# Mixing narrow and wide weight blocks one by one in a two-layer decoder trunk

## Chip, cores and metric

The kernel runs on one core of one Trainium2 chip. The metric is device time in microseconds of one execution; lower is better. Three timed runs of the kernel before gave 772.72, 772.83 and 772.97 us.

## What is computed

A hidden state of 256 tokens by 1024 channels goes through two layers, all in float32. Layer 0 mixes tokens with a gated short convolution, layer 1 with dilated attention. Behind each mixer come a squared-ReLU MLP (1024 to 4096 to 1024) and a gated per-layer embedding.

```python
def short_conv_mixer(h, w_in, w_conv, w_out):
    gate_b, gate_c, xin = jnp.split(h @ w_in, 3, axis=-1)
    y = gate_b * causal_depthwise_conv(gate_c * xin, w_conv)
    return y @ w_out

for i in range(DEPTH):            # DEPTH = 2
    hn = rmsnorm(h, norm_mix[i])
    mixed = short_conv_mixer(hn, ...) if i == 0 else dilated_attention_mixer(hn, positions, ...)
    h = h + mixed
    h = h + squared_relu_mlp(rmsnorm(h, norm_mlp[i]), mlp_w_up[i], mlp_w_down[i])
    ple_gate = jax.nn.sigmoid(rmsnorm(h, norm_ple[i]) @ ple_w_gate[i])
    h = h + ple_gate * (p[i] @ ple_w_proj[i])
return rmsnorm(h, norm_final)
```

## The kernel before

**Split products.** Every float32 operand is split into a high and a low part (`hi`, `lo`), and a product is hi*hi + hi*lo + lo*hi. ScalarE (ACT) writes the high part of the weights (`whi`, L363), VectorE (DVE) the low part (`wlo`, L302). Weights arrive in slabs of up to eight tiles of 128x128. The split buffers hold six slabs, so the split of a slab can start only when TensorE (PE) is done with the slab six before it.

**Blocks.** A block is one 128x128 weight tile against 256 tokens. `block` (L374) issues it in one of these forms. A *narrow* block ("n") is three matmuls of 256 columns into one half of a PSUM bank. A *wide* block ("w") is one matmul of 256 columns (`wlo` against the high part of x) and one of 512 (`whi` against high and low part side by side) into a bank of its own; afterwards `sums` (L414) adds the two halves of that bank, with an ACT copy and a DVE addition for each of the two column blocks. In "w" every second block (`half`) has its two matmuls in reverse order, so that two of 512 columns stand behind each other, and then two of 256. A third form ("t") has the tokens as stationary operand and is not touched.

**The plan.** `make_plan` writes out one list for the whole program: blocks, and steps ("do", ...) such as `conv`, `mix_out`, `gate_out`, `squares`, `stat`. A scheduler then sets each engine's order from that list; each engine runs its own order strictly. Steps named in `URGENT` (L33) go ahead of others. The stages are: the input product of the convolution (`conv_in`, matrices C, B and X, four column pairs c), its output product (`mix`, four column pairs j), the MLP of layer 0 (`mlp_plan`), the gate (`gate_plan`), attention with the products of q, k and v, its output product (`w_o`), the MLP of layer 1, and the last gate.

**The norms.** `h_ready` (L437) makes the operand x of the next product from h[j]: two ACT and two DVE instructions, and then, but for the first norm, `squares` (an ACT square, one or two DVE additions). When the four squares are summed, `stat` (L477) or `stat_rows` (L494) takes the sum over channels with a small matmul. `gate_out(j)` (L632) multiplies the gate's product by a row of norm factors, takes the sigmoid, multiplies, adds to h, and calls `h_ready(3, j)`; attention's first product reads that x3_j. `mix_out(1, j)` (L609) makes x4_j for the MLP of layer 1 in the same way.

Of the kernel before, what the change touches and what calls it, by code (L numbers as in the profile page):

```python
# [49 lines left out]

def head_start(key, name, operand, out, stat=None):

    plan = []
    for kp in range(NP):
        if stat and kp == NP - 2:
            plan.append(("do", "stat", stat))
        for j in (0, 1):
            for k in (2 * kp, 2 * kp + 1):
                for i in (0, 1):
                    plan.append(("w", key, k, 2 * j + i, (name, j), i, operand))  # L60
            if stat and kp == NP - 1 and j == 0:
                plan.append(("do", "spread", stat))
    return plan + [("do", *out, 0), ("do", *out, 1)]


def mlp_plan(layer):
    up, down, x = f"up{layer}", f"down{layer}", f"x{3 * layer + 1}"
    plan = head_start(up, "u", x, ("up_out",))
    for j in range(2, FF // P // 2):
# [4 lines left out]
        if j == 3:  # L74
            plan.append(("do", "stat_rows", 3 * layer + 1))
        if (layer, j) == (0, 8):
# [62 lines left out]
def make_plan():  # L139
# [3 lines left out]
    def conv_in(what, c, ks):  # L143
        s = "BCX".index(what)
        return [
            ("w" if c > 1 and (what, c) != ("B", 3) or what == "X" else "n", "sc_in", k, s * NK + 2 * c + i, (what, c), i, "x0")
# [4 lines left out]
    for kp in range(NP):  # L151
        for what in "CBX":
            plan += conv_in(what, 0, (2 * kp, 2 * kp + 1))
            if what == "C" and kp + 1 < NP:
                plan.append(("do", "x_in", kp + 1))
            if what == "B":
                plan.append(("do", "squares", 0, kp))
    plan.append(("do", "add_up", ("X", 0)))
    for c in range(1, NP):
        plan += conv_in("C", c, range(2))  # L160
        plan += [("do", "stat", 0)] if c == 1 else []
        plan += conv_in("C", c, range(2, NK)) + ([("do", "add_up", ("C", c))] if c > 1 else []) + conv_in("X", c, range(3))
        plan += [("do", "spread", 0), ("do", "conv", 0)] if c == 1 else []
# [3 lines left out]
    def mix(key, j, ks):  # L167
        return [("n", key, k, 2 * j + i, ("o", j), i, "y") for k in ks for i in (0, 1)]

    for k in range(6):  # L170
        plan += mix("sc_out", 0, (k,)) + mix("sc_out", 1, (k,))
    for j in range(NP):
        plan += mix("sc_out", j, range(6 if j < 2 else 0, NK)) + [("do", "mix_out", 0, j)]
# [37 lines left out]
    def w_o(kj):  # L211

        return [
            ("w" if j < 2 else "n", "w_o", k, 2 * j + i, ("o", j), i, "y") for k, j in kj for i in (0, 1)
        ]


    plan += w_o((k, j) for k in range(3) for j in range(3)) + [("do", "scores", last)]
    plan += w_o([(k, j) for k in (3, 4) for j in range(3)] + [(k, 3) for k in range(5)]) + [("do", "turn", last)]
    plan += w_o((5, j) for j in range(NP)) + [("do", "last_values")]  # L220
# [40 lines left out]
def tile_trunk(ctx: ExitStack, tc: tile.TileContext, plan, slabs, ap, out):  # L261
# [54 lines left out]
    for op in plan:  # L316
        if op[0] != "do":
            key = ((*op[4], op[5]), 0) if op[0] == "w" else (op[4], op[5] if op[0] == "n" else 0)
# [55 lines left out]
    def block(kind, key, k, col, name, half, operand, m=0, cuts=1):  # L374
        name = (*name, half) if kind == "w" else name
# [10 lines left out]
        elif kind == "w":  # L386
# [4 lines left out]
            products = products[::-1] if half and (key != "qkv" or col[1] or not col[2]) else products  # L391
# [45 lines left out]
    def h_ready(n, j):  # L437
# [7 lines left out]
        if n:  # L445
# [142 lines left out]
    def conv(c):  # L588
# [5 lines left out]
        pb = sums(("B", c), b) if c == 2 else close(("B", c))  # L594
# [353 lines left out]
```

## Time and profile before

| | |
|---|---|
| median of 3 runs | 772.83 us (772.72 to 772.97) |
| the profiled execution | 772.91 us; its span from first to last instruction 771.1 us |
| PE (matmul), busy | 762.9 us, 99%, 4828 instructions |
| PE weight load, busy | 686.6 us, 89% |
| DVE, busy | 595.4 us, 77% |
| ACT, busy | 483.8 us, 63% |
| DMA | 140.84 MB, 183 GB/s |

The ends of matmuls are modelled and neighbours overlap in the pipeline. So this document reads PE by the distance from one matmul's start to the next, not by busy time.

### The profile page before, as it was taken

The numbers are of one execution on the slowest core, as the hardware profiler recorded it, in microseconds if no ns is written. First come the engines' busy times: TensorE is split into PE (matmuls) and PEld (weight loads), VectorE is DVE, ScalarE is ACT, GpSimd is POOL, SyncE is SP. The second block draws the span as 40 slices with busy tenths as digits, with TensorE's granted clock in tenths as the row PEclk, the third lists the DMA queues.
The fourth block names the chain that finished last, engine by engine and source line by source line (L and its number), as shares of the span: only waits on it lengthen the run. The fifth ranks groups of instructions, "written<-read, shape, count | busy, mean of one in ns | idle before, by whom it ended". The sixth has DMA issues, their size and how long they took to land. (4 is left out here: it accounts for less than half of the span.)

```text
span 771.1 us, 12612 instructions
## 1 busy us (share of the span) xinstructions
PE 762.9 (99%) x4828; PEld 686.6 (89%) x4828; DVE 595.4 (77%) x953; ACT 483.8 (63%) x782; POOL 8.9 (1%) x22
## 2 busy tenths in 40 slices
PE   9999999999999999999999999999999999999996
PEld 9998998888888899989989989989988888888885
DVE  6898779898566668898988978977798887555664
ACT  7655565565444446688887778777575555444454
POOL 0000000000000000000000000000000000000002
PEclk9999999999999999999999999999999999999999
DMA  8855555555555554554556456446456555555521
GB/s 304 311 199 188 188 180 186 189 189 194 190 191 191 189 186 145 185 189 149 174 169 195 151 166 191 154 157 220 137 178 203 193 191 187 184 188 191 185 91 56
DMA packets 42541, 140.84 MB, mean 183 GB/s; under 512 B 4849, under 2 KB 6385, under 8 KB 42481
## 3 DMA queue, kind: packets, MB, share of 16 engines
q1 hardware_dynamic: 41904, 139.39, 53.5%
q8 instruction: 38, 0.62, 0.3%
q10 hardware_dynamic: 576, 0.66, 0.3%
q14 instruction: 23, 0.18, 0.1%
HBM read 138.97 MB, written 1.05 MB: 182 GB/s over the span
## 5 line engine op out<-in xcount | busy, mean ns | idle before, releaser
L302 DVE TENSOR_TENSOR wlo<-raw,whi 128x1024 fp32r<-128x1024 f32 (+2 forms) x277 | 319.4, 1156 | 135.4 <-ACT whi L363 132.6
L363 ACT ACTIVATE whi<-raw 128x1024 fp32r<-128x1024 f32 (+2 forms) x277 | 278.0, 1007 | 183.4 <-PE acc_d L399 77.1
L399 PE MATMUL acc_u<-x,whi 128*128 128x512 f32 x512 | 160.8, 396 | 0.0
L399 PE MATMUL acc_d<-u,whi 128*128 128x512 f32 x512 | 160.8, 395 | 0.0
L399 PE MATMUL acc_qk<-x,whi 128*128 128x512 f32 x384 | 124.6, 395 | 0.0
L399 PEld LDWEIGHTS acc_d<-u,wlo 128*128 128x128 f32 x512 | 96.2, 188 | 22.7
L399 PEld LDWEIGHTS acc_u<-x,wlo 128*128 128x128 f32 x512 | 96.0, 188 | 22.8 <-ACT x L442 0.4
L399 PE MATMUL acc_u<-x,wlo 128*128 128x256 f32 x512 | 101.6, 278 | 0.1
L399 PE MATMUL acc_d<-u,wlo 128*128 128x256 f32 x512 | 100.9, 278 | 0.0
L399 PE MATMUL acc_qk<-x,wlo 128*128 128x256 f32 x384 | 86.9, 280 | 0.0
L399 PEld LDWEIGHTS acc_qk<-x,wlo 128*128 128x128 f32 x384 | 72.1, 188 | 12.1
L399 PEld LDWEIGHTS acc_u<-x,whi 128*128 128x128 f32 x512 | 78.0, 189 | 0.2
L399 PEld LDWEIGHTS acc_d<-u,whi 128*128 128x128 f32 x512 | 77.9, 189 | 0.0
L399 PE MATMUL acc_v<-whi,x 128*128 128x384 f32 x256 | 67.2, 337 | 0.0
L399 PEld LDWEIGHTS acc_qk<-x,whi 128*128 128x128 f32 x384 | 62.5, 188 | 4.6
L399 PEld LDWEIGHTS acc_v<-whi,x 128*128 128x128 f32 x256 | 46.5, 188 | 0.1
L399 PE MATMUL acc_o<-y,whi 128*128 128x256 f32 (+1 forms) x224 | 44.7, 299 | 0.0
L399 PE MATMUL acc_v<-wlo,x 128*128 128x384 f32 x128 | 42.9, 335 | 0.0
L418 ACT ACTIVATE r<-acc_u 128x256 f32<-128x256 f32 x64 | 23.8, 373 | 24.6 <-PE acc_u L399 24.4
L650 ACT ACTIVATE rot<-qk 16x512 f32<-16x512 f32 x48 | 30.3, 632 | 9.9 <-DVE qk L419 9.2
L399 PEld LDWEIGHTS acc_o<-y,whi 128*128 128x128 f32 x224 | 34.8, 191 | 0.0
L399 PE MATMUL acc_o<-y,wlo 128*128 128x256 f32 x128 | 33.7, 284 | 0.0
(175 smaller groups left out, 976.7 us busy)
## 6 DMA issues: line engine op xcount, KB each, us to landing
raw<-in_w SPq DMA_DIRECT2D x230, 512.0 KB, 3.3
raw<-in_w SPq DMA_DIRECT2D x32, 384.0 KB, 3.6
raw<-in_w SPq DMA_DIRECT2D x10, 256.0 KB, 5.3
h<-in_xT SPq DMA_DIRECT2D x4, 256.0 KB, 5.5
gain<-in_gain SPq DMA_DIRECT2D x2, 256.0 KB, 4.6
out<-htg SPq DMA_DIRECT2D x2, 256.0 KB, 2.1
mask<-in_mask SPq DMA_DIRECT2D x2, 192.0 KB, 4.1
raw<-in_w ACTq DMA_DIRECT2D x2, 128.0 KB, 4.2
```

What stands on the lines that cost most here:

```text
L302: nc.vector.tensor_tensor(out, a, f32(b), ALU.subtract)
L363: nc.scalar.activation(hi[:, :width], t[:, :width], AF.Copy)
L399: nc.tensor.matmul(to, a, b, start=n == 0 and name not in opened, stop=n == len(products) - 1 and left[name, half if kind == "n" else 0] == 0,
L418: nc.scalar.activation(t[:, i, :], p[:, 1, :], AF.Copy)
L650: nc.scalar.activation(r[dst : dst + 16], p[src : src + 16], AF.Copy)
```

## The change

Four things change in the plan. (1) In the convolution's input product, blocks of B (narrow now for every c) and X are taken in turn by a new helper `mixed`; C stays a run of its own. (2) In the convolution's output and in the gate, half of the column pairs become wide (j = 0 and 3, and j = 0 and 2), and wide and narrow blocks are taken in turn; in attention's output the existing wide and narrow blocks are taken in turn. (3) The wide blocks of these stages have a new kind "m": as "w", but always with 256 columns first. (4) `h_ready` no longer calls `squares` for norms 1 and 4 (those of the MLPs); the plan calls it behind `up_out(2)` to `up_out(5)`, and `stat_rows` comes after j = 7 and not 3.

```diff
+def mixed(*lists):
+    at = [((n + 0.5) / len(x), m, op) for m, x in enumerate(lists) for n, op in enumerate(x)]
+    return [op for _, _, op in sorted(at, key=lambda e: e[:2])]
 def mlp_plan(layer):
...
-        if j == 3:
+        if j < 2 + NP:
+            plan.append(("do", "squares", 3 * layer + 1, j - 2))
+        if j == 3 + NP:
             plan.append(("do", "stat_rows", 3 * layer + 1))
 def gate_plan():
     def gate(j, ks):
-        return [("n", "gate0", k, 2 * j + i, ("g", j), i, "x2") for k in ks for i in (0, 1)]
+        return [("n" if j % 2 else "m", "gate0", k, 2 * j + i, ("g", j), i, "x2") for k in ks for i in (0, 1)]
-    plan = gate(0, range(6)) + gate(1, range(4)) + [("do", "stat", 2)] + gate(1, (4, 5)) + gate(0, (6, 7))
+    plan = mixed(gate(0, range(6)), gate(1, range(4))) + [("do", "stat", 2)] + mixed(gate(0, (6, 7)), gate(1, (4, 5)))
     plan += [("do", "spread", 2), ("do", "gate_out", 0)] + gate(1, (6, 7)) + [("do", "gate_out", 1)]
-    return plan + [x for j in (2, 3) for x in (*gate(j, range(NK)), ("do", "gate_out", j))]
+    plan += mixed(gate(2, range(NK)), gate(3, range(5))) + [("do", "gate_out", 2)]
+    return plan + gate(3, range(5, NK)) + [("do", "gate_out", 3)]
 def make_plan():
...
-            ("w" if c > 1 and (what, c) != ("B", 3) or what == "X" else "n", "sc_in", ...)
+            ("m" if what == "X" else "w" if what == "C" and c > 1 else "n", "sc_in", ...)
...
-        plan += conv_in("X", c, range(3, NK)) + [("do", "add_up", ("X", c))] + conv_in("B", c, range(NK))
-        plan.append(("do", "conv", c))
+        bx = mixed(conv_in("B", c, range(NK)), conv_in("X", c, range(NK)))
+        plan += bx[:6] + ([("do", "spread", 0), ("do", "conv", 0)] if c == 1 else [])
+        plan += bx[6:] + [("do", "add_up", ("X", c)), ("do", "conv", c)]
...
+        return [("n" if j in (1, 2) else "m", "sc_out", k, 2 * j + i, ("o", j), i, "y") for k in ks for i in (0, 1)]
+    plan += mixed(mix(0, range(6)), mix(1, range(6)), mix(2, range(4)))
+    plan += mixed(mix(0, (6, 7)), mix(1, (6, 7)), mix(2, (4, 5))) + [("do", "mix_out", 0, 0), ("do", "mix_out", 0, 1)]
+    plan += mixed(mix(2, (6, 7)), mix(3, range(4))) + [("do", "mix_out", 0, 2)]
+    plan += mix(3, range(4, NK)) + [("do", "mix_out", 0, 3)]
...
-            products = products[::-1] if half and (key != "qkv" or col[1] or not col[2]) else products
+            products = products[::-1] if kind == "w" and half and (key != "qkv" or col[1] or not col[2]) else products
...
-        if n:
+        if n not in (0, 1, 4):
             squares(n, j)
...
     def gate_out(j):
         s = act(f"gs{j}")
-        nc.vector.tensor_tensor(s, close(("g", j)), both(rows[2]), ALU.mult)
+        g = close(("g", j)) if ("g", j) in acc else sums(("g", j), s)
+        nc.vector.tensor_tensor(s, g, both(rows[2]), ALU.mult)
```

In the first part of the convolution's input product, PE's order was the following; `acc_B` and `acc_X` are the accumulators of matrices B and X.

```order
L399 MATMUL acc_B_253<-x_0_164,wlo_192 128x256
L399 MATMUL acc_B_253<-x_0_164,whi_191 128x256 x2
L399 MATMUL acc_X_0_274<-x_0_164,wlo_214 128x256
L399 MATMUL acc_X_0_274<-x_0_164,whi_213 128x512
L399 MATMUL acc_X_1_287<-x_0_164,whi_213 128x512
L399 MATMUL acc_X_1_287<-x_0_164,wlo_214 128x256
```

It is now:

```order
L414 MATMUL acc_B_253<-x_0_164,wlo_192 128x256
L414 MATMUL acc_B_253<-x_0_164,whi_191 128x256 x2
L414 MATMUL acc_X_0_261<-x_0_164,wlo_192 128x256
L414 MATMUL acc_X_0_261<-x_0_164,whi_191 128x512
L414 MATMUL acc_B_253<-x_0_164,wlo_192 128x256
L414 MATMUL acc_B_253<-x_0_164,whi_191 128x256 x2
L414 MATMUL acc_X_1_267<-x_0_164,wlo_192 128x256
L414 MATMUL acc_X_1_267<-x_0_164,whi_191 128x512
```

Four matmuls of 256 columns now stand between two of 512; before, X's blocks stood in pairs and B's in runs.

At the end of the gate, DVE's order from `gate_out(2)` to x3_3 was the following; `gs` are the gates, `hr` the new h, `x3_j` the low part of attention's operand, `tot` the sums of squares.

```order
L634 TENSOR_TENSOR gs2_3253<-acc_g_2_3192,row_2_3145 128x512
L455 TENSOR_TENSOR tot3_1_3189<-tot3_1_3189,tot3_0_3161 128x256
L302 TENSOR_TENSOR wlo120_3356<-raw120_3193,whi120_3355 128x1024
L636 TENSOR_TENSOR gs2_3253<-gs2_3253,prj2_223 128x512
...
L302 TENSOR_TENSOR wlo122_3405<-raw122_3271,whi122_3404 128x768
L636 TENSOR_TENSOR gs3_3331<-gs3_3331,prj3_231 128x512
L642 TENSOR_TENSOR hr3_3335<-h3_86,gs3_3331 128x256 x2
L302 TENSOR_TENSOR wlo123_3427<-raw123_3301,whi123_3426 128x768
L443 SCALAR_TENSOR_TENSOR x3_3_3338<-hr3_3335,gains_73,x3_3_3338 128x256 x2
```

It is now:

```order
L317 TENSOR_TENSOR wlo120_3325<-raw120_3173,whi120_3324 128x1024
L434 TENSOR_TENSOR gs2_3261<-acc_g_2_0_3172,gs2_3261 128x256
L434 TENSOR_TENSOR gs2_3261<-acc_g_2_1_3185,gs2_3261 128x256
L650 TENSOR_TENSOR gs2_3261<-gs2_3261,row_2_3121 128x512
L317 TENSOR_TENSOR wlo121_3351<-raw121_3200,whi121_3350 128x768
L652 TENSOR_TENSOR gs2_3261<-gs2_3261,prj2_223 128x512
...
L317 TENSOR_TENSOR wlo123_3396<-raw123_3250,whi123_3395 128x768
L652 TENSOR_TENSOR gs3_3300<-gs3_3300,prj3_231 128x512
L658 TENSOR_TENSOR hr3_3304<-h3_86,gs3_3300 128x256 x2
L317 TENSOR_TENSOR wlo124_3418<-raw124_3322,whi124_3417 128x768
L458 SCALAR_TENSOR_TENSOR x3_3_3307<-hr3_3304,gains_73,x3_3_3307 128x256 x2
```

Two additions stand ahead of gate 2's chain, and every gate stands one slab's split later in the order: split 120 comes before the first instruction of gate 2, and split 124 and not 123 is the last one ahead of x3_3. The bank of `acc_g_2_0` is the next one that attention's accumulator `acc_qk_0_2_1` takes; before, that accumulator took the bank of `acc_g_1`.

ACT's order at the beginning of that chain, behind the row of norm factors (`row_2`), was:

```order
L363 ACTIVATE whi115_3126<-raw115_2981 128x1024
L512 ACTIVATE row_2_3145<-spread_2_3142 128x256
L635 ACT_TABLE_LOAD
L635 ACTIVATE gs0_3147<-gs0_3147 128x512
L363 ACTIVATE whi116_3195<-raw116_3021 128x1024
```

It is now:

```order
L378 ACTIVATE whi115_3104<-raw115_2972 128x1024
L433 ACTIVATE gs0_3123<-acc_g_0_0_3011 128x256
L433 ACTIVATE gs0_3123<-acc_g_0_1_3024 128x256
L527 ACTIVATE row_2_3121<-spread_2_3118 128x256
L378 ACTIVATE whi116_3175<-raw116_3012 128x1024
L651 ACT_TABLE_LOAD
L651 ACTIVATE gs0_3123<-gs0_3123 128x512
```

Two copies for `sums` are added, and the split of slab 116 stands ahead of the table load and the first sigmoid, no longer behind it. In PE's order at x3_3's first use, three matmuls of 256 columns that need only its high part stand ahead of the first that needs the low part (one before), and `stat(3)` stands behind four blocks of that x and not two.

## Rows read from the trace of the kernel before

**Rows 1.** The page's busy times by engine, and the answer on what PE waited for: engine, line, what it waited for, then us in total, times, longest.

```profile
PE 762.9 (99%) x4828; PEld 686.6 (89%) x4828; DVE 595.4 (77%) x953; ACT 483.8 (63%) x782; POOL 8.9 (1%) x22
PE warm L526 <- DVE power L522: 1.0, 1, 1.0
```

**Rows 2.** Stretches of the span: the convolution's output (narrow blocks alone) and the MLP of layer 0 (wide ones alone). Columns: from and to, length, then busy us and count of PE, PE's weight load, DVE, ACT and POOL, then granted clock, DMA share and GB/s.

```profile
80.10:103.10 23.00, 23.00 (x194) 23.00 (x193) 19.23 (x29) 13.86 (x20) 0.00 (x0) 1.00 0.51 184
103.10:281.70 178.60, 178.60 (x1028) 155.86 (x1027) 128.44 (x174) 95.13 (x135) 0.00 (x0) 1.00 0.55 189
```

**Rows 3.** Timeline of PE (start, us, what), first and last row of a run of narrow blocks: one row of wlo per block, 14 blocks from the first to the last.

```profile
41.08 0.28 PE L399 MATMUL acc_B<-x,wlo 128*128 128x256 f32 x1
...
46.12 0.28 PE L399 MATMUL acc_B<-x,wlo 128*128 128x256 f32 x1
```

**Rows 4.** The same of wide blocks in paired order (two of 256, two of 512): six blocks between these two rows.

```profile
47.06 0.39 PE L399 MATMUL acc_C<-x,wlo 128*128 128x256 f32 x2
...
49.15 0.40 PE L399 MATMUL acc_C<-x,wlo 128*128 128x256 f32 x2
```

**Rows 5.** The same of wide blocks in plain order (256, 512, 256, 512, in attention): 15 blocks between these two rows.

```profile
332.00 0.28 PE L399 MATMUL acc_qk<-x,wlo 128*128 128x256 f32 x1
...
337.20 0.27 PE L399 MATMUL acc_qk<-x,wlo 128*128 128x256 f32 x1
```

**Rows 6.** Timeline of PE in attention's output, where two narrow blocks already follow four wide ones in paired order; a round of six blocks goes from one matmul pair of 512 columns at its beginning to the next.

```profile
527.95 0.62 PE L399 MATMUL acc_o<-y,whi 128*128 128x512 f32 x2
...
529.12 0.39 PE L399 MATMUL acc_o<-y,wlo 128*128 128x256 f32 x2
...
529.94 0.28 PE L399 MATMUL acc_o<-y,wlo 128*128 128x256 f32 x1
530.05 0.63 PE L399 MATMUL acc_o<-y,whi 128*128 128x512 f32 x2
...
532.17 0.63 PE L399 MATMUL acc_o<-y,whi 128*128 128x512 f32 x2
```

**Rows 7.** Timeline of ACT at the beginning of the chain of gates (brackets: idle before it, and what ended that).

```profile
291.07 1.06 ACT L363 ACTIVATE whi<-raw 128x1024 fp32r<-128x1024 f32 x1 [2.27 <-PE acc_g L399]
292.90 0.38 ACT L512 ACTIVATE row<-spread 128x256 f32<-128x256 f32 x1 [0.77 <-PE spread L508]
293.30 1.28 ACT L635 ACT_TABLE_LOAD   x1
294.60 0.63 ACT L635 ACTIVATE gs<-gs 128x512 f32<-128x512 f32 x1
295.13 1.05 ACT L363 ACTIVATE whi<-raw 128x1024 fp32r<-128x1024 f32 x1
```

**Rows 8.** Timeline of DVE along the chain of gates, from the squares of the gate's own norm to x3_3.

```profile
288.29 0.43 DVE L455 TENSOR_TENSOR tot<-tot,tot 128x256 f32<-128x256 f32 x1
...
295.26 0.69 DVE L636 TENSOR_TENSOR gs<-gs,prj 128x512 f32<-128x512 f32 x1 [1.25 <-ACT gs L635]
...
306.46 0.68 DVE L634 TENSOR_TENSOR gs<-acc_g,row 128x512 f32<-128x512 f32 x1
...
315.94 0.94 DVE L302 TENSOR_TENSOR wlo<-raw,whi 128x768 fp32r<-128x768 f32 x1
316.80 0.86 DVE L443 SCALAR_TENSOR_TENSOR x<-hr,gains,x 128x256 fp32r<-128x256 f32 x2
...
318.03 0.43 DVE L455 TENSOR_TENSOR tot<-tot,tot 128x256 f32<-128x256 f32 x1
```

**Rows 9.** Timeline of PE from the gate's small matmuls to `stat(3)`: the second of the two matmuls in the row at 308.56 is the first into acc_qk_0_2_1; the row at 318.32 begins with the first that needs the low part of x3_3.

```profile
288.94 0.51 PE L481 MATMUL ssq<-ones,tot 128*128 128x2 f32 x4
...
292.26 0.60 PE L508 MATMUL spread<-ident,n 128*128 128x128 f32 x4
...
305.66 0.28 PE L399 MATMUL acc_qk<-x,wlo 128*128 128x256 f32 x1
...
308.56 0.63 PE L399 MATMUL acc_qk<-x,whi 128*128 128x512 f32 x2
...
318.32 0.63 PE L399 MATMUL acc_qk<-x,whi 128*128 128x512 f32 x2
...
318.90 0.50 PE L481 MATMUL ssq<-ones,tot 128*128 128x2 f32 x4
```

**Rows 10.** Timeline at the beginning of the MLP of layer 1: PE, and DVE's low part of x4_1.

```profile
555.15 0.28 PE L399 MATMUL acc_u<-x,wlo 128*128 128x256 f32 x1
...
558.75 0.62 PE L399 MATMUL acc_u<-x,whi 128*128 128x512 f32 x2
559.22 0.99 PE L399 MATMUL acc_u<-x,wlo 128*128 128x256 f32 x4
560.10 0.73 PE L399 MATMUL acc_u<-x,whi 128*128 128x512 f32 x2
560.67 0.40 PE L399 MATMUL acc_u<-x,wlo 128*128 128x256 f32 x2
...
559.56 0.89 DVE L443 SCALAR_TENSOR_TENSOR x<-hr,gains,x 128x256 fp32r<-128x256 f32 x2 [0.15 <-ACT x L442]
```

**Rows 11.** DVE additions and ACT copies of `sums`, from the timelines in attention's output.

```profile
551.97 0.77 DVE L419 TENSOR_TENSOR so<-acc_o,so 128x256 f32<-128x256 f32 x2 [1.16 <-ACT so L418]
551.56 0.73 ACT L418 ACTIVATE so<-acc_o 128x256 f32<-128x256 f32 x2 [1.67 <-PE acc_o L399]
```

More of the change, by code (lines that the diff above doesn't have):

```diff
@@ L145, in conv_in @@
         return [
-            ("w" if c > 1 and (what, c) != ("B", 3) or what == "X" else "n", "sc_in", k, s * NK + 2 * c + i, (what, c), i, "x0")
+            ("m" if what == "X" else "w" if what == "C" and c > 1 else "n", "sc_in", k, s * NK + 2 * c + i, (what, c), i, "x0")
             for k in ks for i in (0, 1)
@@ L151, in make_plan @@
     for kp in range(NP):
[L152 to L157, printed above, removed]
+        ks = (2 * kp, 2 * kp + 1)
+        plan += conv_in("C", 0, ks)
+        if kp + 1 < NP:
+            plan.append(("do", "x_in", kp + 1))
+        bx = mixed(conv_in("B", 0, ks), conv_in("X", 0, ks))
+        plan += bx[:4] + [("do", "squares", 0, kp)] + bx[4:]
     plan.append(("do", "add_up", ("X", 0)))
@@ L161, in make_plan, with mix @@
         plan += [("do", "stat", 0)] if c == 1 else []
-        plan += conv_in("C", c, range(2, NK)) + ([("do", "add_up", ("C", c))] if c > 1 else []) + conv_in("X", c, range(3))
-        plan += [("do", "spread", 0), ("do", "conv", 0)] if c == 1 else []
-        plan += conv_in("X", c, range(3, NK)) + [("do", "add_up", ("X", c))] + conv_in("B", c, range(NK))
-        plan.append(("do", "conv", c))
[L167 to L173, printed above, removed]
+        plan += conv_in("C", c, range(2, NK)) + ([("do", "add_up", ("C", c))] if c > 1 else [])
+        bx = mixed(conv_in("B", c, range(NK)), conv_in("X", c, range(NK)))
+        plan += bx[:6] + ([("do", "spread", 0), ("do", "conv", 0)] if c == 1 else [])
+        plan += bx[6:] + [("do", "add_up", ("X", c)), ("do", "conv", c)]
+    def mix(j, ks):
+        return [("n" if j in (1, 2) else "m", "sc_out", k, 2 * j + i, ("o", j), i, "y") for k in ks for i in (0, 1)]
[3 more added lines that the diff above has]
+    plan += mix(3, range(4, NK)) + [("do", "mix_out", 0, 3)]
     plan += mlp_plan(0) + gate_plan()
@@ L213, in w_o, with wide @@
         return [
-            ("w" if j < 2 else "n", "w_o", k, 2 * j + i, ("o", j), i, "y") for k, j in kj for i in (0, 1)
+            ("m" if j < 2 else "n", "w_o", k, 2 * j + i, ("o", j), i, "y") for k, j in kj for i in (0, 1)
         ]
-    plan += w_o((k, j) for k in range(3) for j in range(3)) + [("do", "scores", last)]
-    plan += w_o([(k, j) for k in (3, 4) for j in range(3)] + [(k, 3) for k in range(5)]) + [("do", "turn", last)]
-    plan += w_o((5, j) for j in range(NP)) + [("do", "last_values")]
+    def wide(ks):
+        return w_o([(k, j) for k in ks for j in (0, 1)])
+    plan += mixed(wide(range(3)), w_o((k, 2) for k in range(3))) + [("do", "scores", last)]
+    plan += mixed(wide((3,)), w_o((k, 2) for k in (3, 4))) + mixed(wide((4,)), w_o((k, 3) for k in range(5)))
+    plan += [("do", "turn", last)] + mixed(wide((5,)), w_o((5, j) for j in (2, 3))) + [("do", "last_values")]
     for j in range(NP):
@@ L374, in block @@
     def block(kind, key, k, col, name, half, operand, m=0, cuts=1):
-        name = (*name, half) if kind == "w" else name
+        name = (*name, half) if kind in "wm" else name
         if name not in opened:
@@ L593, in conv @@
         pc = cur.pop(("C", c)) if c > 1 else close(("C", c))
-        pb = sums(("B", c), b) if c == 2 else close(("B", c))
+        pb = close(("B", c))
         nc.vector.tensor_tensor(t, pc, both(rows[0, 2]), ALU.mult)
```

6 lines of the change are left out of this document (3 added, 3 removed).

## Prediction

> **What bounds the kernel now.** I read the page's busy times, then PE's waits, then PE's timeline in runs of one kind of block, and last the timelines of DVE and ACT where the PE needs their results soonest. PE is busy for 99% of the span and waits for another engine only at its very first matmul [rows 1]. Since matmul ends are modelled, a short wait could hide in that 99%; the starts tell. They stand in even steps nearly everywhere, at full granted clock [rows 2], so a change moves the time in two ways: it changes the length of those steps, or it makes an operand come late at one of the few places with little slack.
>
> The steps: a narrow block takes (46.12 - 41.08) / 14 = 0.360 us [rows 3], so 0.120 per matmul of 256 columns. A wide block in paired order takes (49.15 - 47.06) / 6 = 0.348 [rows 4], one in plain order (337.20 - 332.00) / 15 = 0.347 [rows 5].
>
> The thin places: the gate's sum of squares is done at 288.29 + 0.43 = 288.72, and PE uses it at 288.94 [rows 8, 9], 0.22 later. The first half of the low part of x3_3 is ready near 317.25 (start 316.80, half of 0.86), and PE needs it at 318.32, 1.1 later. And x4_1 comes too late: behind 559.22 four matmuls of 256 take 0.88 where they should take 0.47, and the two of 512 behind them 0.57 where 0.47 is usual; PE loses 0.51 us there while DVE makes x4_1 from 559.56 [rows 10].
>
> **Term A, kinds of block.** 32 blocks of the convolution's output and 32 of the gate become wide, 16 of B become narrow: net 48 blocks at 0.360 become 48 at 0.347 or 0.348. That is -0.6 us. Columns streamed are the same; what goes is 48 matmuls, 13 ns each, which is what a matmul costs above its columns: 0.120 less 256 columns at 2.4 GHz, 0.107 [rows 3]. The Trainium skill ("TensorE: Matmul & The Clock Gate", Back-to-back issue gap) puts that extra at 2.5 ns for a warm matmul; by it A would be an estimated -0.1 us, and the trace, with 13 ns, disagrees.
>
> **Term B, taking them in turn.** In the new order, which I counted through, there are some 125 places where a single 512 is followed by three or more matmuls of 256. No stretch of before has that order. Nearest is attention's output, where two narrow blocks follow four paired wide ones [rows 6]: its rounds take 2.10 and 2.12 us, and the parts apart would be 4 x 0.348 + 2 x 0.360 = 2.11. Within a round the seven steps from 529.12 take 0.82, 0.117 each, 3 ns below 0.120, but the 512s are that much longer. So I bound B by nothing and by 3 ns for four matmuls at each place, 125 x 0.012 = -1.5 us, and take a third, -0.5, since whole rounds gain almost nothing.
>
> **Term C, the MLP of layer 1.** Without `squares` in `h_ready`, DVE and ACT have less to do ahead of x4_1. But the new order also asks for x4_1 sooner: eight blocks of u0 and u1 come first and only three matmuls of 256 and one of 512 before its low part is needed, near 555.15 + 3.4, where before twelve blocks came first. DVE's new order has, behind the last matmul of the old product at 555.15, two additions to h at 0.6, one slab's split at 1.15 and then x4_1's first half at 0.45, with 0.25 for the matmul to end and 0.6 of x4_0 left over: ready near 555.15 + 3.6. So most of the 0.51 us goes: -0.4, bounds -0.5 and +0.1.
>
> **Term D, from the gate into attention.** This is the term that decides. Times are in the clock of before, with the end of the MLP in place.
> - PE reaches `stat(2)` after 12 wide and 8 narrow blocks, 7.05 us and not 7.2, so 0.15 sooner; the slack of 0.22 covers that.
> - `spread` then comes at 292.0 (292.26 less 0.15 and four wide blocks' 0.05, and some of B), and PE is through four more blocks near 293.9. Only then is the buffer for the split of slab 116 free: ACT's splits start some 0.25 behind PE, as that of 115 at 291.07 does [rows 7]. So ACT splits from 294.15 to 295.1, and now the table load (1.3) and the sigmoid (0.63) stand behind it: the sigmoid ends near 297.0, and DVE's second multiplication of gate 0 starts near 297.1. Before, table load and sigmoid came first and it started at 295.26 [rows 7, 8]. The chain is 1.8 late.
> - From 295.26 to 316.80 DVE shows no idle time, four gates one behind the other with eight slab splits between; so lateness stays. Added are gate 2's two additions, 0.77 [rows 11]; the last split in the chain is a short one of 768 in place of one of 1024, 0.27 less. Sum: +2.3.
> - The first addition of gate 2 frees the bank of acc_qk_0_2_1. Its place follows what was at 306.46 by 1.8 and one addition of squares: it ends near 308.9 to 309.0. PE, with a gate that is 0.43 shorter by its wide blocks and 0.1 by B, wants the bank at 308.80 - 0.55 = 308.25. Wait: 0.7 us.
> - x3_3's low part is ready near 317.25 + 2.3 = 319.5. PE wants it at 318.32 - 0.55 + 0.7, and 0.24 later for the two matmuls that now stand ahead: 318.7. Wait: 0.8 us. `stat(3)`, four blocks on at 320.8, finds its sum ready: 1.2 behind x3_3's first half, as before (318.46 against 317.25) [rows 8].
>
> D is +1.5 us. Its bounds: +0.3, if my lags on ACT are each some tenths too long, and +4.3, if the chain misses one more slab's release (below).
>
> **At no cost.** Squares moved behind `up_out(2)` to (5): one ACT square and two DVE additions for each of four steps, under 1.5 us of each engine's time per step, where DVE is idle for 50 of 178.6 us [rows 2]; if that cover were gone, some 0.9 us of DVE per step would reach PE. The convolution: X's sums now begin when B and X end together, some 2 us later, but 32 blocks (11 us) and not 24 (8.6 us) lie ahead of the first that needs its y. The new `sums` of the convolution's output run beside 20 blocks (7 us).
>
> **Sum.** -0.6 - 0.5 - 0.4 + 1.5 = 0.0 against the profiled execution's 772.91 us (span 771.1 and 1.8 around it). The median of the timed runs is 0.08 below that execution, so the forecast is 772.8.
>
> **Rivals.**
> - *The wait behind the gate stays hidden.* If ACT's split of 116 finds its buffer before the row of norm factors comes, the table load is where it was and D is near 0: 771.3. For it: DVE idles 1.25 us at 295.26, room for the two additions of gate 0 [rows 8]. Against it: slab 110 ends behind the four narrow blocks after `spread`, by the plan. With B at its far end this gives 770.3.
> - *Slower: one more slab missed.* The splits of 122 and 124 stand ahead of the high parts of x3_2 and x3_3 in ACT's order, and each waits for PE to finish a slab, eight blocks or 2.8 us. If the late chain meets such a release too late, x3_3 comes 2.8 later still: 775.6. It decides once the waits pass 1.5 + 1.55 = 3.1 us. Against it: by my times the splits of 122 and 124 have their buffer 0.3 us or more before DVE's h is there.
> - *The alternation does nothing* (B = 0, C = 0): 773.7. For it: whole rounds of 2.10 and 2.12 against 2.11 [rows 6].
> - *The narrow matmuls are bound by their weight loads, and the long ones give the loads time.* For it: the load path is busy 23.00 of 23.00 us in the narrow stretch and 155.86 of 178.60 in the wide one [rows 2], and one step of 256 ahead of a 512 shows 0.11 (529.94 to 530.05) [rows 6]. At that step for four matmuls at each place the gain is 125 x 4 x 0.010 = 5 us: 767.8. Against it: the other steps there are 0.117, and in plain wide order, where each load has a long matmul near it, a block still costs 27 ns above its 768 columns [rows 5]. The Trainium skill (same page, What happens when you issue a matmul) has loads pulled ahead of matmuls in flight into a background buffer; that agrees with both readings.
>
> **How the numbers follow.** No change that a measurement of this kernel can tell is one within 0.2%, 1.55 us: 771.3 to 774.4. Chances: forecast 0.50 (own range 771.4 to 774.0, from A's, B's and C's bounds and tenths on D), hidden 0.18, one more slab 0.16, nothing from alternation 0.10, loads 0.06. Hidden lies on the bound, so half of it counts as faster, with the loads and 0.05 of the forecast: 0.20. Slower: 0.16 and some 0.04 of the edges, 0.20. The rest, 0.60, is the same. The range runs from 770.6 to 774.6: it leaves out the loads' case and most of the slab's.
>
> **What would show it.** Right: at the first acc_qk matmuls of head 0 a gap of some 0.7 us about three us into attention, and one of 0.8 where x3_3 is first used; ACT's split ahead of a table load near 295; no gap in the first 6 us of layer 1's MLP; blocks of 256 in mixed order near 0.117 to 0.120 each. Wrong: no gap into attention (then faster by 1.5), gaps over 3 us (slower), or steps of 256 near 0.11 all through the mixed stretches.

## The result, and the profile after

The changed kernel takes 773.99 us (773.67 to 774.28), the kernel before 772.86 (772.26 to 773.29), 20 runs each: a ratio of 1.0014, 95% interval 1.0008 to 1.0021. Its profiled execution has a span of 772.0 us, before 771.1. I had forecast no change, 772.8. The time lies in my range, but the change is slower beyond the interval.

The page's busy times after, and then the answer on what PE waited for (us in total, times, longest), to be held against [rows 1]:

```profile
PE 762.8 (99%) x4780; PEld 683.5 (89%) x4780; DVE 595.9 (77%) x959; ACT 486.5 (63%) x788; POOL 8.9 (1%) x22
```

```profile
PE warm L541 <- DVE power L537: 1.0, 1, 1.0
PE acc_qk L414 <- DVE gs L434: 0.6, 1, 0.6
PE acc_qk L414 <- DVE x L458: 0.4, 1, 0.4
```

There are 48 matmuls fewer, as counted, and two new waits, both on DVE and both just into attention. PE's timeline there, against [rows 9]:

```profile
308.26 0.39 PE L414 MATMUL acc_qk<-x,whi 128*128 128x512 f32 x1
309.26 0.47 PE L414 MATMUL acc_qk<-x,whi 128*128 128x512 f32 x1 [0.61 <-DVE gs L434]
309.56 0.40 PE L414 MATMUL acc_qk<-x,wlo 128*128 128x256 f32 x2
...
318.62 0.77 PE L414 MATMUL acc_qk<-x,wlo 128*128 128x256 f32 x4
319.80 0.73 PE L414 MATMUL acc_qk<-x,whi 128*128 128x512 f32 x2 [0.41 <-DVE x L458]
320.37 0.40 PE L414 MATMUL acc_qk<-x,wlo 128*128 128x256 f32 x2
...
321.18 0.50 PE L496 MATMUL ssq<-ones,tot 128*128 128x2 f32 x4
```

Read the starts, not only the brackets. One matmul of 512 stands between 308.26 and 309.26: 1.00 us where 0.23 is usual, 0.77 lost. Four of 256 stand between 318.62 and 319.80: 1.18 where 0.47 is usual, 0.71 lost. The step behind each restart is long as well: one of 512 takes 0.30 (309.26 to 309.56), and two take 0.57 where 0.47 is usual (319.80 to 320.37), 0.07 and 0.10 more. Together that is 1.65, so each wait costs more than its bracket says.

The chain behind it, first ACT's timeline and then DVE's, against [rows 7, 8]:

```profile
294.23 1.06 ACT L378 ACTIVATE whi<-raw 128x1024 fp32r<-128x1024 f32 x1 [1.11 <-PE acc_g L414]
295.31 1.28 ACT L651 ACT_TABLE_LOAD   x1
296.60 0.63 ACT L651 ACTIVATE gs<-gs 128x512 f32<-128x512 f32 x1
```

```profile
297.27 0.69 DVE L652 TENSOR_TENSOR gs<-gs,prj 128x512 f32<-128x512 f32 x1 [0.72 <-ACT gs L651]
308.69 0.75 DVE L434 TENSOR_TENSOR gs<-acc_g,gs 128x256 f32<-128x256 f32 x2
319.26 0.88 DVE L458 SCALAR_TENSOR_TENSOR x<-hr,gains,x 128x256 fp32r<-128x256 f32 x2
```

ACT's split of slab 116 now precedes the table load, the sigmoid ends near 297.2, and DVE's second multiplication of gate 0 starts at 297.27 where it started at 295.26. By these rows it is two microseconds late there and 2.46 late at x3_3 (319.26 against 316.80). The MLP of layer 0 ends 0.10 sooner in this trace than in that of before, so in the clock of before each is 0.10 later still.

Cutting both traces at the starts of the same PE matmuls shows where the time went (lengths in us). I call the fifth stretch, from the gate into attention, the seam:

| from the first matmul of | before us | after us | difference |
|---|---|---|---|
| the convolution | 68.70 | 69.20 | +0.50 |
| its output | 23.04 | 22.80 | -0.24 |
| MLP of layer 0 | 178.60 | 178.60 | 0.00 |
| the gate | 23.92 | 23.72 | -0.20 |
| the seam: qk of head 0, to `spread(3)` | 19.29 | 20.91 | +1.62 |
| attention from there | 202.89 | 202.88 | -0.01 |
| attention's output (last) | 27.31 | 27.36 | +0.05 |
| MLP of layer 1 | 179.14 | 178.62 | -0.52 |

The sum is +1.2, the medians differ by 1.13; the start-up ahead of the convolution differs by some tenths from one profiled execution to the next, whatever the kernel (11.0 to 11.7). Stretches that no edit touches agree to 0.02 between the traces, with one exception: the convolution's part ahead of `spread(0)` took 25.39 in the kernel before and 25.72 in a later run with the same convolution. So up to some 0.2 of the convolution's +0.50 may be scatter; from `spread(0)` on it went from 43.32 to 43.62, +0.30. Against my terms: D was forecast at +1.5 and is 1.62. C was forecast at -0.4 and is -0.52; the stall of [rows 10] is gone, the four matmuls of 256 take 0.47:

```profile
559.17 0.64 PE L414 MATMUL acc_u<-x,wlo 128*128 128x256 f32 x4
559.64 0.86 PE L414 MATMUL acc_u<-x,whi 128*128 128x512 f32 x3
```

A and B together were forecast at -1.1, and the four mixed stages make +0.1 (0.50 - 0.24 - 0.20 + 0.05). That is the miss, whole but for the scatter. A mixed stretch looks like this (convolution, after; a wide block of X and a narrow one of B by turns):

```profile
42.03 0.28 PE L414 MATMUL acc_B<-x,wlo 128*128 128x256 f32 x1
...
42.74 0.28 PE L414 MATMUL acc_B<-x,wlo 128*128 128x256 f32 x1
...
43.45 0.28 PE L414 MATMUL acc_B<-x,wlo 128*128 128x256 f32 x1
```

A pair of blocks takes 0.71 us; apart, by [rows 3, 4], they would take 0.360 + 0.348 = 0.708. My first reading was that a 512 alone among 256s costs 3 ns extra. The runs in plain order below speak against that.

### The profile page after: what moved, and what is told of

The parts are those of the page before. It is cut to its first block, busy times and chain, and to the rows that moved or that the text cites. A ratio compares the mean times of both kernels' runs of the same rounds, so it can differ in the third digit from the quotient of the medians.

```text
span 772.0 us, 12534 instructions
## 1 busy us (share of the span) xinstructions
PE 762.8 (99%) x4780; PEld 683.5 (89%) x4780; DVE 595.9 (77%) x959; ACT 486.5 (63%) x788; POOL 8.9 (1%) x22
## 3 DMA queue, kind: packets, MB, share of 16 engines
HBM read 138.97 MB, written 1.05 MB: 181 GB/s over the span
## 4 chain that ended last, share of the span: by engine, by line
PE 95%; DVE 3%; issue 1%; POOL 0%; ACT 0%; POOLq 0%; DVEq 0%
PE acc_u L414 23%; PE acc_d L414 23%; PE acc_qk L414 16%; PE acc_v L414 9%; PE acc_o L414 6%; PE acc_g L414 4%; PE acc_C L414 3%; PE acc_B L414 3%; PE acc_X L414 3%; PE acc_p L414 1%; DVE wlo L317 1%; PE sc L703 1%; PE o L747 1%; PE o L757 1%; PE sc L711 1%
## 5 line engine op out<-in xcount | busy, mean ns | idle before, releaser
L414 PE MATMUL acc_o<-y,wlo 128*128 128x256 f32 x128 | 36.0, 284 | 0.0
L414 PEld LDWEIGHTS acc_o<-y,whi 128*128 128x128 f32 x192 | 31.7, 189 | 2.8
```

The costliest lines, as they stand in the source:

```text
L414: nc.tensor.matmul(to, a, b, start=n == 0 and name not in opened, stop=n == len(products) - 1 and left[name, half if kind == "n" else 0] == 0,
```

## Experiments

### The gate put back

The changed kernel with `gate_plan` as a whole as in the kernel before, its first line for one:

```diff
-        return [("n" if j % 2 else "m", "gate0", k, 2 * j + i, ("g", j), i, "x2") for k in ks for i in (0, 1)]
+        return [("n", "gate0", k, 2 * j + i, ("g", j), i, "x2") for k in ks for i in (0, 1)]
...
```

> The changed kernel with the gate's blocks alone put back: all narrow, in the order of before. Theory (the loss sits at the seam from the gate into attention, because norm factors, ACT's table load and DVE's chain of gates run 1.8 us late there): the two waits that PE shows at the first acc_qk matmuls (0.61 us for DVE's gs, 0.41 us for x) go, 1.6 us are won there, the gate takes 0.2 us more, the attention after it starts at the same place as in the kernel before or a little sooner: 772.6 us. Rival (the loss is spread over the mixed stretches of the convolution and of attention's output): nothing that can be told, 774.0 us.

Measured: 772.85 us, before in the same runs 772.89 (ratio 0.9999, 0.9990 to 1.0008). PE's only wait is the first one:

```profile
PE warm L540 <- DVE power L536: 1.0, 1, 1.0
```

The seam takes 19.30 us again. So the gate's part of the change accounts for the loss, 773.99 less 772.85 or 1.14, and by the traces the seam alone for more than that; the rest of the change comes out at no difference that can be told.

### The squares alone

On the kernel before. One more line moves with the squares, here and in the changed kernel: `rope`, the rotary angles, comes one j later in the MLP of layer 0. That stage takes 178.59 to 178.60 us either way.

```diff
-        if j == 3:
+        if j in range(2, 2 + NP):
+            plan.append(("do", "squares", 3 * layer + 1, j - 2))
+        if j == 3 + NP:
             plan.append(("do", "stat_rows", 3 * layer + 1))
-        if (layer, j) == (0, 8):
+        if (layer, j) == (0, 9):
             plan.append(("do", "rope"))
...
-        if n:
+        if n not in (0, 1, 4):
             squares(n, j)
```

> The kernel before with one edit: the squares of x1 and x4 move behind the up products, as in the changed kernel. Theory (DVE gets x4_1 done sooner): the stall of 0.5 us at the first use of x4_1 in the MLP of layer 1 goes, nothing else moves: 772.35 us. Rival (the new order of attention's output took the stall away, not the squares): 772.85 us, the stall of 0.5 us still there. Against the claim that squares beside the up products cost nothing: a new wait of PE in either up product.

Measured: 772.55 (before 772.89; 0.9996, 0.9987 to 1.0005). By the times no difference can be told; by the trace the MLP of layer 1 takes 178.71 where it took 179.14, the stall is gone and no new wait is there. So 0.43 us of C come from the squares, and at most the last 0.1 from the new order of attention's output.

### In runs, plain and paired

The changed kernel's blocks in their kinds, first without the mixing, then (last two lines) with the wide ones also in paired order:

```diff
 def mixed(*lists):
-    at = [((n + 0.5) / len(x), m, op) for m, x in enumerate(lists) for n, op in enumerate(x)]
-    return [op for _, _, op in sorted(at, key=lambda e: e[:2])]
+    return [op for x in lists for op in x]
...
-            products = products[::-1] if kind == "w" and half and (key != "qkv" or col[1] or not col[2]) else products
+            products = products[::-1] if half and (key != "qkv" or col[1] or not col[2]) else products
```

> The changed kernel with its kinds of block and the squares as they are, but the lists that were mixed one by one now taken one behind the other. Theory (each 512 alone among matmuls of 256 takes 3 ns more than in a run of wide blocks, some 125 places): the stretches of the convolution, its output and the gate get shorter by 0.3 to 0.4 us together, the waits at the seam stay and eat what the gate gains: 773.7 us. My prediction's term B (mixing saves 0.5 us, at most 1.5): 774.5 us or more. Rival (order makes no difference, the stretches are as long as mixed): 774.0 us.

> The changed kernel in runs (as in the run with the lists one behind the other), and its wide blocks of the convolution, its output, the gate and attention's output in paired order (256, 512, 512, 256) in place of plain order (256, 512, 256, 512). In runs and in plain order a wide block of the output took 0.3525 us by the trace ((22.83 - 32 x 0.360) / 32 = 0.353), not the 0.347 that I took from head 1's qk blocks. Theory (A was mis-sized: plain order costs 0.3505 to 0.3525 in these stages, paired order 0.348): convolution 0.1 to 0.2 us shorter, its output 22.66 us in place of 22.80, the gate 0.1 us shorter: 773.35 us. Rival (order within a block makes no difference, these stages' operands make wide blocks cost that): 773.7 us and the output stays at 22.80 us.

Measured: 773.71 in runs (before 772.89), 773.25 in runs and paired (before 772.98). The intervals of the two ratios overlap (1.0002 to 1.0020 and 0.9994 to 1.0012), so the traces have to decide. From `spread(0)` on the convolution takes 43.62 mixed, 43.69 in runs, 43.42 paired; its output 22.80, 22.83 and 22.67; the gate 23.72, 23.74 and 23.68. So the mixing of single blocks gains 0.02 to 0.07 us in each of these stages over the same blocks in runs, and the order within the wide block is worth some 0.5 us: paired, the three stages take 0.27, 0.16 and 0.06 less. The first run met the time of its theory, 773.7, by luck: the stages did not get shorter, but the seam did, 20.42 us against 20.91, with one wait in place of two. The timeline shows the price of plain order (convolution's output in runs; 14 blocks from the first row to the last):

```profile
98.41 0.28 PE L413 MATMUL acc_o<-y,wlo 128*128 128x256 f32 x1
98.77 0.28 PE L413 MATMUL acc_o<-y,wlo 128*128 128x256 f32 x1
99.12 0.28 PE L413 MATMUL acc_o<-y,wlo 128*128 128x256 f32 x1
99.47 0.28 PE L413 MATMUL acc_o<-y,wlo 128*128 128x256 f32 x1
...
103.36 0.28 PE L413 MATMUL acc_o<-y,wlo 128*128 128x256 f32 x1
```

(103.36 - 98.41) / 14 = 0.3536 us, with steps of 0.36, 0.35, 0.35 over and over. In attention the same order gives 0.347 [rows 5]. That is the price that I carried over, and here it doesn't hold. The theory of 3 ns for each lone 512 fell with the first of these runs: there, wide blocks stand in runs, and the stages are no shorter.

### Pairs by turns

The changed kernel with the gate as before, wide blocks in paired order, and two blocks at a time:

```diff
-    at = [((n + 0.5) / len(x), m, op) for m, x in enumerate(lists) for n, op in enumerate(x)]
+    at = [((n // 2 + 0.5) / len(x), m, op) for m, x in enumerate(lists) for n, op in enumerate(x)]
...
```

> The changed kernel with the gate as before, and in the convolution, its output and attention's output two narrow blocks by turns with two wide ones in paired order (512, 512, 256 and seven more of 256), where the change took single blocks by turns (512, 256, 256, 256, 256). In the run with pairs in the output such a round of four blocks took 1.407 us, and the kinds apart would take 2 x 0.360 + 2 x 0.348 = 1.416. Theory (taking in turn does gain, but only when the wide blocks come in pairs): the output takes 16 x 1.407 = 22.51 us where the changed kernel takes 22.80, the convolution from its second row of factors on 43.3 where that takes 43.62: 772.1 us. Rival (a round gains nothing over runs in paired order): output 22.66, convolution 43.42, 772.5 us.

Measured: 772.27 (before 772.96; 0.9992, 0.9983 to 1.0000), between the theory's time and the rival's. By the trace the convolution from `spread(0)` on takes 43.25, its output 22.59. Against the paired runs that is 0.17 and 0.08 less, so taking in turn does gain something, some 0.25 us in these two stages, once the wide blocks come in pairs. The convolution came out as forecast; the output, at 22.59, missed 22.51; by its plan 8 wide blocks of j = 3 come alone at its end, and narrow and wide are not one to one ahead of them.

### The sigmoid's table loaded early

The changed kernel with a small sigmoid behind the sine, in the first run on `ones` in place of `cosr`:

```diff
         nc.scalar.activation(cosr, k, AF.Sin)
+        early = spool.tile([P, 1], F32, tag="early", name="early")
+        nc.scalar.activation(early, cosr[:, :1], AF.Sigmoid)
```

> The changed kernel with one instruction more: a sigmoid of one column behind the rotary angles' sine, in the MLP of layer 0, so that ACT's table for the sigmoid is loaded there and not behind the split of slab 116. Theory (the table load of 1.28 us stands in the chain that makes the seam late): the first sigmoid of the gate starts 1.3 us sooner, near 295.3, DVE's chain follows by 1.3 us, PE's wait for gs goes, the one for x shrinks to 0.2 us or goes: 772.7 us. Rival (DVE's two additions and its order set the wait, the table load is covered): the waits stay, 774.0 us.

> The changed kernel with one sigmoid of one column that reads the cosine of the rotary angles, so that it can't move ahead of it: the sigmoid's table is loaded in the MLP of layer 0 and not behind the split of slab 116. (In the run before, the small sigmoid had no operand that held it and moved to the start of the kernel; the table was loaded at the gate as ever.) Theory: the first sigmoid of the gate starts 1.3 us sooner, near 295.3, DVE's chain follows, the wait for gs goes, the one for x shrinks to 0.2 us or goes: 772.7 us. Rival (DVE's additions and its order set the waits, the load is covered): 774.0 us.

Measured: 774.12 for the first, which told nothing on the table: its sigmoid ran at 3.4 us, the sine's table replaced it at 172, and the gate loaded its own as ever. The second: 773.50 (before 772.98; the ratio 1.0006, 0.9997 to 1.0014, against the changed kernel's 1.0014, 1.0008 to 1.0021), between theory and rival. The chain there, in a trace whose gate starts 0.39 later than the changed kernel's, on ACT and then on DVE:

```profile
294.62 1.06 ACT L378 ACTIVATE whi<-raw 128x1024 fp32r<-128x1024 f32 x1 [1.11 <-PE acc_g L414]
295.58 0.62 ACT L653 ACTIVATE gs<-gs 128x512 f32<-128x512 f32 x1
```

```profile
295.71 1.23 DVE L317 TENSOR_TENSOR wlo<-raw,whi 128x1024 fp32r<-128x1024 f32 x1 [0.62 <-ACT whi L378]
296.85 0.69 DVE L654 TENSOR_TENSOR gs<-gs,prj 128x512 f32<-128x512 f32 x1
```

Of PE's waits one at acc_qk is left:

```profile
PE acc_qk L414 <- DVE x L458: 0.4, 1, 0.4
```

The sigmoid starts 1.4 us sooner, DVE's multiplication only 0.8 (296.85 - 0.39 against 297.27): DVE's own part of slab 116's split now stands right ahead of it. The wait for gs goes, the one for x stays; the seam shrinks from 20.91 to 20.18. So without the table load 0.8 of the lateness of 2.0 goes, not the 1.3 expected. By these rows the rest is the late split itself, through both engines; no run moved that split alone.

### Gate 2 narrow

On the changed kernel:

```diff
-        return [("n" if j % 2 else "m", "gate0", k, 2 * j + i, ("g", j), i, "x2") for k in ks for i in (0, 1)]
+        return [("n" if j else "m", "gate0", k, 2 * j + i, ("g", j), i, "x2") for k in ks for i in (0, 1)]
```

> The changed kernel with gate 2 narrow as before, gate 0 wide: DVE's two additions for gate 2, 0.75 us, fall away, 16 blocks of the gate take 0.1 to 0.15 us more. Theory (these additions are part of the chain of DVE from the gate into attention, 0.77 of 2.3 us): the wait at the first acc_qk matmuls goes, of the 1.6 us lost at the seam 0.8 remain at x3_3: 773.3 us. Rival (only ACT's table load sets the seam): 774.1 us.

Measured: 773.29 (before 772.98; 1.0005, 0.9996 to 1.0014). The time is the one forecast, the place is not: x3_3 was to keep a loss of 0.8, but both waits at acc_qk are gone, and a new one stands at the small matmuls of `stat(3)`, for the sum of squares:

```profile
PE ssq L496 <- DVE tot L470: 0.4, 1, 0.4
```

The seam takes 19.86, so 0.56 of the 1.62 remain, for 0.14 more in the gate itself (23.86). By the traces the two additions' 0.75 us of DVE are worth more at the seam than the table load, 1.05 us against 0.73; the times of the two runs are too close to tell them apart.

### Squares and pairs: what the parts are worth without the gate

On the kernel with the squares alone:

```diff
-        return [("n", key, k, 2 * j + i, ("o", j), i, "y") for k in ks for i in (0, 1)]
+        return [("w" if j in (0, 3) else "n", key, k, 2 * j + i, ("o", j), i, "y") for k in ks for i in (0, 1)]
```

> The kernel before with the squares behind the up products, and with the convolution's output in the order of before but wide in paired order for j = 0 and 3. The gate is that of before. Theory (the squares are worth 0.3 to 0.5 us, 32 paired wide blocks 32 x 0.012 = 0.38 us, and there is no seam to lose at): 772.15 us, the output's stage 22.66 us in place of 23.04. Rival (the wide blocks' sums make x1 late, or a wide block in this stage costs what a narrow one does): 772.5 us or more.

Measured: 772.18 (before 772.98; 0.9989, 0.9980 to 0.9997). The output's stage takes 22.61, against 22.66 expected. This is the lowest median of the versions, faster than the kernel before by a tenth of a per cent; the run with pairs by turns, 772.27, can't be told from it. A round of two wide and two narrow blocks there takes (84.92 - 80.70) / 3 = 1.407, where the kinds apart take 1.416:

```profile
80.70 0.63 PE L401 MATMUL acc_o<-y,whi 128*128 128x512 f32 x2
...
84.92 0.63 PE L401 MATMUL acc_o<-y,whi 128*128 128x512 f32 x2
```

### Plain order has two prices

Four runs on the last kernel, with the MLPs' wide blocks in plain order. In three of them, at some places, three blocks are issued as 256, 256, 256, 512, 512, 512: in every j of up from 2 on and of down; in up's j = 2; in up's j = 2 and 9, with the first two j of up left paired. `hold` is true for both blocks of k = 1 and the first of k = 2 in the j named.

```diff
-            products = products[::-1] if half and (key != "qkv" or col[1] or not col[2]) else products
+            products = products[::-1] if half and key[:2] not in ("up", "do") and (key != "qkv" or col[1] or not col[2]) else products
...
+            if hold and n:
+                later.append(issue)
+            else:
+                issue()
+        if len(later) == 3:
+            while later:
+                later.pop(0)()
```

> The kernel with the squares moved and the output in pairs, with both MLPs' 768 wide blocks each in plain order in place of paired order. By the traces a wide block in plain order takes 353.9 ns in the convolution, its output and the gate, in a pattern that repeats every three blocks, and 346.6 ns in attention, in one that repeats every two. Theory one (the pattern is set by what the run of plain blocks is entered from, and only narrow blocks before it give the slow one): 346.6 ns throughout, each up product 0.2 us shorter, some 2.5 us less in all: 769.5 us. Theory two (the slow pattern belongs to these stages, the fast one to attention): 353.9 ns in both MLPs, 1,500 blocks at 5.5 ns, some 8 us more: 780 us. A third outcome: the fast pattern in one MLP and not in the other.

> The kernel with both MLPs' wide blocks in plain order (512 each, not 768 as I wrote of the run before), and once in each j of up (from 2) and down three blocks taken as 256, 256, 256, 512, 512, 512. In the run before, MLP 0 went by the slow pattern throughout (353.3 ns a block), MLP 1 changed to the fast one (346.7) behind three 512s in a row near 561.5 us and kept it to its end; its times fell into two groups, near 773.8 and near 777.0. Theory (the same code has two steady patterns; a place with three 512s in a row can turn the slow into the fast, which then lasts): with such a place every 16 or 64 blocks nearly all of both MLPs goes at 346.7, 1024 x 1.7 ns under the paired order: 770.5 us, one group of times. Rival (what turned it was something else, and three 512s in a row turn it back as often): between 773 and 777, spread out.

> As the run before it, but with one such place only in each MLP, in up's j = 2. Theory: each MLP goes by one pattern from there on, fast or slow, so times fall into groups 1.7 to 3.4 us apart, and the fastest is near 770.7 us; where the turn always succeeds there, one group at 770.7. Rival (the pattern does not last without being renewed): a time between that of the run with many places and 777.

> The kernel with the squares moved and the output in pairs; in both MLPs the first two j of up stay in paired order, the rest of up and all of down go in plain order, with three 512s in a row only in up's j = 2 and j = 9, that is where the runs before had just gone into the slow pattern (from the head and from the two matmuls of the sum of squares). In the run with such a place in every j they turned slow into fast and the next one fast into slow, by turns. Theory (a place with three 512s turns a steady slow run into the fast pattern, which lasts until the next other form of matmul): in each MLP 96 blocks of up from j = 2 and some 350 from j = 9 on at 346.7, 16 at 353.3: 450 x 1.7 ns less, 0.7 us each MLP: 770.8 us. Rival (which pattern follows such a place depends on where in the slow pattern's three blocks it falls, so either may come): an MLP, or a part of it, at 353.3 from such a place on; with both wrong throughout 776.7 us.

All plain: 776.95 us, but in two groups, 773.71 and 773.91, and four times 776.94 to 777.39. (The MLPs have 512 wide blocks each; the first expectation says 768.) The profiled execution was of the shorter group. This is the third outcome named in the expectation, one price in one MLP and the other in the other. The MLP of layer 0 has 123 blocks between the first two rows below, that of layer 1 has 123 between the last two:

```profile
103.32 0.28 PE L401 MATMUL acc_u<-x,wlo 128*128 128x256 f32 x1
146.78 0.28 PE L401 MATMUL acc_u<-x,wlo 128*128 128x256 f32 x1
...
561.36 0.28 PE L401 MATMUL acc_u<-x,wlo 128*128 128x256 f32 x1
561.48 0.86 PE L401 MATMUL acc_u<-x,whi 128*128 128x512 f32 x3
562.18 0.28 PE L401 MATMUL acc_u<-x,wlo 128*128 128x256 f32 x1
...
602.98 0.28 PE L401 MATMUL acc_u<-x,wlo 128*128 128x256 f32 x1
645.62 0.28 PE L401 MATMUL acc_u<-x,wlo 128*128 128x256 f32 x1
```

43.46 / 123 = 0.3533 against 42.64 / 123 = 0.3467: the same code, operands of the same shape, two steady patterns of steps. By these prices I estimate that an execution with both MLPs in the long pattern takes 3.3 us more (some 500 blocks at 0.0067), about what parts the two groups; no execution of the longer group was profiled. The change came behind three 512s in a row at 561.48, which the scheduler had made there by itself. With such a place in every j (773.62, 773.43 to 773.98) the pattern turned from long to short at one and mostly back at the next, by turns; the 770.5 us of the theory were missed. With one place (775.91, 775.54 to 776.41, one group and not several) it turned short at up's j = 2 in layer 0 and went long again behind the two matmuls of the sum of squares:

```profile
145.67 0.39 PE L406 MATMUL acc_u<-x,whi 128*128 128x512 f32 x1
...
147.06 0.39 PE L406 MATMUL acc_u<-x,whi 128*128 128x512 f32 x1
147.29 0.40 PE L506 MATMUL ssq<-sums,ones_r 128*128 128x256 f32 x2
...
147.64 0.40 PE L406 MATMUL acc_u<-x,whi 128*128 128x512 f32 x1
...
148.70 0.40 PE L406 MATMUL acc_u<-x,whi 128*128 128x512 f32 x1
```

Four blocks ahead of the two take 1.39 (0.347 each), three behind them 1.06 (0.353). In layer 1 the pattern was long ahead of the place and stayed long behind it.

With places at the two entries only, j = 2 and 9: 773.86, in groups of 770.83 to 771.72 (five) and 773.81 to 774.84 (seven). Its profiled execution, of the long group, shows the short pattern behind j = 9 in layer 0 (105 blocks at 0.3467 between the first two rows) and the long one behind the same place in layer 1 (99 blocks at 0.3533 between the last two):

```profile
156.08 0.28 PE L406 MATMUL acc_u<-x,wlo 128*128 128x256 f32 x1
192.48 0.28 PE L406 MATMUL acc_u<-x,wlo 128*128 128x256 f32 x1
...
608.00 0.28 PE L406 MATMUL acc_u<-x,wlo 128*128 128x256 f32 x1
642.98 0.28 PE L406 MATMUL acc_u<-x,wlo 128*128 128x256 f32 x1
```

Behind j = 2 both layers went long; ahead of j = 9 the pattern was long in layer 0 and short in layer 1, so that place turned it over in both. The rival was right: either may follow. The best execution took 770.83, the theory's 770.8, but no execution of that group was profiled, and the version can't be relied on. What inside PE decides stays open. Shown is that a pattern, once entered, lasts until matmuls of another form come, that two matmuls of 256 or a row of 512s can turn it, and that the same program can go either way.

## Why the prediction was wrong, point by point

- **What bounds the kernel.** Right: by the table the time moved with lengths of steps and with late operands at thin places. PE is busy for 99% after as before.
- **Term A failed.** The step was "32 of the output and 32 of the gate at 0.360 become 0.347 or 0.348", and the change of X's and attention's output's wide blocks from paired to plain order got no term at all. The 0.347 came from attention [rows 5], a stretch in the short pattern. In the stages that changed, plain blocks in runs take 0.3536; mixed singly, a pair of blocks takes 0.71, so a wide one some 0.350. At that price X's 64 blocks cost 0.1 to 0.2 more than paired ones and B's 16 narrow ones 0.19 more, as counted, which together is about the convolution's +0.30; the output and the gate gain 0.24 and 0.20 where 32 x 0.013 = 0.42 each was forecast. With paired blocks the output's gain is there: 22.61 to 22.67 against 23.04. The kernel before has no plain run outside attention, and there every one steps at 0.347, so its trace could not show the other price; that I took one stretch for all was the error.
- **Term B failed, in size.** Single blocks by turns save 0.1 us in all over the same blocks in runs, not 0.5, and they take 0.4 to 0.5 more than runs in paired order. [Rows 6], on which I built, has paired blocks; with pairs by turns some 0.25 us are there. The change took the pairs apart, and I carried the row over as if it hadn't.
- **Term C held**: -0.52 where -0.4 was forecast, a little past its bound of -0.5; -0.43 of it with the squares alone.
- **Term D held** in its places and causes; that its size fits so well is partly luck. In the clock of before, the sigmoid's end was forecast at 297.0 and came at 297.3; DVE's multiplication at 297.1 and 297.4; the bank at 308.9 to 309.0, and PE went on at 309.36. So the chain was 0.3 to 0.4 later than I had it. But PE, too, wanted the bank 0.3 later than forecast (308.6, not 308.25), because the gate got 0.20 shorter and not 0.5: that is the error of terms A and B again. The two errors cancel in the waits, 0.7 and 0.8 forecast, 0.77 and 0.71 measured. The weights within the chain were wrong: without the table load 0.73 of the 1.62 go, without gate 2's additions 1.05. I had the chain 1.8 late by the split ahead of the load and 0.77 by the additions; but the split stays late on both engines when the load is gone.
- **Squares at no cost**: held, no wait in either up product.
- **The rivals.** "The alternation does nothing" (773.7, chance 0.10) was nearest by its number, and that is partly luck: it had B near nothing rightly, but C at nothing, which was wrong by 0.5, and it kept A. The waits were neither hidden, nor did the chain miss one more slab, and weight loads gave nothing back: in the mixed stretch shown above the steps of 256 are 0.116 to 0.124.
- **The signs of being right** all came: both gaps, the split ahead of the table load, no gap in layer 1's MLP, steps of 256 near 0.117 to 0.120. They tested C, D and the case of the loads; none of them tested the price of a wide block, on which A rested.

## What to carry to other kernels

A step length read from one stretch is the price of that stretch: before it is multiplied by the blocks of another, look for a second stretch of the same order, and see whether steps repeat every two blocks or every three. Prefer an order with one price (here paired, 256, 512, 512, 256, at 0.348 to 0.350 in every run of it without a wait) to one that is at times 2 ns better and at times 5 ns worse. And what is won ahead of a chain without slack is lost at it: here PE came 0.2 us sooner out of the gate, the added sums made the chain later, and both went into the same wait.

## What was not expected of the hardware

- Matmuls with 256 and 512 columns in strict alternation run in one of two steady patterns at full granted clock: 0.3467 us a pair, repeating every two pairs, or 0.3533 to 0.3536, repeating every three. In the kernel before, all seven plain runs in attention step at 0.347. The MLPs of one kernel can differ in it, and so can two executions (773.8 and 777.0 us for the same program).
- Two blocks of each kind by turns take 1.407 us where the kinds apart take 1.416 and single blocks by turns 1.42.
- The bracket on a waiting matmul is less than what the wait costs: 0.61 and 0.41 in brackets, 0.77 and 0.71 by the starts up to the restart, and 0.07 and 0.10 more in the step behind it.
